# Second batch's four gate projections in a stage of their own, as a 2x2 block product with seven multiplications

## The chip, the cores and the metric

One core of one Trainium2 chip. Matmuls run on TensorE (PE in the profile), elementwise work on VectorE (DVE), ScalarE (ACT) and GpSimd (POOL); SyncE (SP) only issues DMAs. The metric is device microseconds of one execution, as the median of several; the profile is of one execution.

## The reference

Two independent inputs x of 1024 positions x 1024 channels (here: batch 0 and batch 1) go through one layer. The input is normalised and multiplied by one large projection; the result is cut into the sections fv (Fourier branch), fg (its gate), three parts of hv (Hyena branch), hg (its gate) and mg (two merge gates).

```python
xn = rmsnorm(x, g_pre)
p = xn @ w_in
fv, fg, hv, hg, mg = jnp.split(p, [...], axis=-1)
...
y_f = (fz * jax.nn.silu(fg)) @ w_fourier_out
hv = short_conv(hv, w_short)
v, x1, x2 = jnp.split(hv, 3, axis=-1)
...
for n, gate in enumerate((x1, x2)):
    z = gate * long_conv(z, kf[:, n], hyena_d[n])
y_h = (z * jax.nn.silu(hg)) @ w_hyena_out
g_f, g_h = jnp.split(jax.nn.sigmoid(mg + b_merge), 2, axis=-1)
out = (g_f * y_f + g_h * y_h) @ w_out
return x + rmsnorm(out, g_post)
```

The short convolution has width 3 over the positions; the long convolution has a filter as long as the sequence, computed by a small network from the positions, and is done by a Fourier transform of twice the length. Everything is in float32.

## The kernel before

**Precision and matmuls.** A float32 operand is split into two rounded parts, high and low (`split`, L168: ScalarE rounds the high part, VectorE or GpSimd subtracts it). A product is three matmuls, high x high, high x low and low x high (`mm3`, L365), accumulated in a PSUM tile of 128 x 512. All go through `mm` (L192), so the profile shows them under L193 and tells them apart by the PSUM tile's name; subtractions and other two-operand work stand under L181, the three-operand form under L177, the roundings under L171.

**Phases.** `phase_fourier` computes the Fourier branch of both batches and stores the normalised, transposed input in DRAM (`d_x`: 8 tiles of 128 channels x 1024 positions) and the branch's result in `d_fz`. `phase_main` computes the filters' spectra for 8 channel tiles and 2 orders (`filter_taps`, `filter_spectrum`), filling TensorE in between with gate projections of batch 0, and then calls `branches`. `phase_out` does the output projections.

**A projection** (`inproj`, L707) makes one channel tile of 128 output channels for all 1024 positions: two PSUM tiles (`pin0`, `pin1`, 512 positions each), contraction over 8 input tiles, three matmuls each, 48 in all. The weight comes in two halves of 256 KB by SP's queue, is rounded by ScalarE (`wh`) and the rest is subtracted by GpSimd (`wl`). The moving operands are the input's parts `xh0` to `xh7` and `xl0` to `xl7`, loaded by `load_x` (L694) once for each batch; each of these 16 tiles exists once, so batch 1's are loaded when batch 0's last projection has read them. Sections 1 to 3 are the convolution inputs v, x1 and x2, section 0 is the Fourier gate, 4 the Hyena gate, 5 and 6 the two merge gates.

**The branches** (`branches`, L886). For each batch there are 16 steps (n, c): long convolution n of channel tile c, in the order (0,0), (0,1), (1,0), (0,2), (1,1) ... (1,7). A step has a short convolution `conv` (L723: a projection, two scaled copies on ScalarE, four three-operand instructions on VectorE), two of them where n is 0; then `conv_front` (L757: two sums, eight transposes `tph`, the butterfly of VectorE work with its splits `bh`, `bl`); then `conv_back` (L771), which for four groups of frequencies does the forward matmuls (`pX`, four or twelve), VectorE's product with the filter spectrum (`t`, two of 128 x 512; `y`, two of 128 x 256; the split `yh`, `yl`) and twelve inverse matmuls (`pT`), and then joins the groups (`S`, `T1s`, `U`, `T0s`, `ez`, `q`, `yc`); and `gate` (L844), the product with x1 or x2 and the filter's norm `invn`. The result z of n = 1 goes to DRAM (`d_sh`). The x tiles have four buffers, so projections can run ahead of the convolutions by a few steps.

**The gate projections.** Batch 0's stand mostly between the filter computations (`spill_gate`, L739, which stores section 5 and 6 as they are, and section 0 as silu times `d_fz`, in `d_g`). In the branches batch 0 has only section 4 for channel tiles 6 and 7 left. Batch 1 has all of them in the branches: section 4 in `gates` (L904), where GpSimd multiplies x2 by silu of the projection ahead of the convolution, and sections 0, 5 and 6 by `spill_gate` behind each step with n = 1. These are 32 projections.

**Order.** A scheduler orders each engine's instructions at build time from a model of their times; each engine then runs its list in order, waiting on semaphores.

**Output phase** (`phase_out`, L940): for each batch and half of the positions, `operand` loads and splits the eight f tiles (`d_g[b][0]`) and h tiles (`d_sh[b]`), and 8 x 24 matmuls each for `pyf` and `pyh`, the merge gates and the last projection (`po`) follow. The first unit's f tiles are loaded into the pools `sp` and `op`, the others into the tiles of the input x.

Of the kernel before, what the change touches and what calls it, by code (L numbers as in the profile page):

```python
# [16 lines left out]
P = 128  # L17
# [144 lines left out]
class K:  # L162
# [28 lines left out]

    def mm(self, out, lhsT, rhs, start, stop):  # L192
        self.nc.tensor.matmul(out, lhsT, rhs, start=start, stop=stop)  # L193

# [170 lines left out]
    def mm3(self, out, L_, R_, start, stop):  # L365

        self.mm(out, L_[0], R_[0], start, False)
        self.mm(out, L_[0], R_[1], False, False)
        self.mm(out, L_[1], R_[0], False, stop)

# [400 lines left out]
    def conv_back(self, n, ct, B, ws):  # L771
# [3 lines left out]
        for g, pairs in GROUPS:  # L775
# [22 lines left out]
            for r in range(2):  # L798
                for i, pr in enumerate(pairs):
# [12 lines left out]
                    else:  # L812
                        out = T4[:, 1:3]
                        R = [ci[:, hl, o:o + 2 * P].rearrange("p (a b) -> p a b", a=2) for hl in range(2)]
                    self.mm3(out, w, R, i == 0, i == 1)

# [69 lines left out]
    def branches(self, nb, nct, ws):  # L886

        nc = self.nc  # L890
        steps = []
# [12 lines left out]
        def gates(i):  # L904
            b, n, c = steps[i]
            x = self.conv(2 + n, c, ws, f"x{n + 1}")
            if n:
                early = b == 0 and c < NH
                ps = None if early else self.inproj(4, c)
                for q in range(2):  # L910
                    sg = self.wp.tile([P, 512], F32, tag="gt", name="sg", bufs=3)
                    if early:
                        nc.sync.dma_start(sg, self.d_g[0][4][c][:, 512 * q:512 * q + 512])
                    nc.scalar.activation(sg, sg if early else ps[q], AF.Silu)
                    self.mul("pool", x[:, 512 * q:512 * q + 512], x[:, 512 * q:512 * q + 512], sg)
            X[i] = x
        B = front(0)
        gates(0)
        for i, (b, n, c) in enumerate(steps):
# [13 lines left out]
            if b == 0 and NF <= c:  # L933
                self.spill_gate(0, 0, c, ws)
            if b:
                for sec in (0, 5, 6):
                    self.spill_gate(b, sec, c, ws)


    def phase_out(self):  # L940
# [5 lines left out]
        with ExitStack() as es:  # L946
            pool = lambda n: es.enter_context(tc.tile_pool(name=n, bufs=1, reuse_waits="tile"))
            oc, sp, op = pool("oc"), pool("sp"), pool("op")
            wo = {}
            self.nw = 0  # L950

            def operand(i, nm, k):


                b, half = units[i]
                src = (self.d_sh[b] if nm == "h" else self.d_g[b][0])[k][:, 512 * half:512 * half + 512]
                if nm == "f" and i == 0:
                    h = sp.tile([P, 512], F32R, tag=f"mh{k}", name=f"sf{k}", bufs=1)
                    if k % 2 == 0:
                        self.pair = op.tile([P, 2, 512], F32R, tag="xo"[k // 2 % 2], name="sl", bufs=2)  # L960
                    l = self.pair[:, k % 2]
                    r = l.bitcast(F32)
                    nc.sync.dma_start(r, src)
                    self.split(h, l, r, "dve", "act")
                    return h, l
                t = xp.tile([P, 2, 512], F32R, tag=f"x{'l' if nm == 'h' else 'h'}{k}", name=f"s{nm}{k}", bufs=1)
                r = t[:, 1].bitcast(F32)
# [46 lines left out]
            for i, (b, half) in enumerate(units):  # L1014
# [20 lines left out]
                for tt in range(4):  # L1035
                    c = slice(P * tt, P * tt + P)
                    row = 512 * half + P * tt
                    x = op.tile([P, D], F32, tag="x", name="xr", bufs=2)
                    nc.sync.dma_start(x, a[f"x{b}"][row:row + P, :])
# [4 lines left out]
                          for n in range(2)]  # L1044
                    o = op.tile([P, D], F32, tag="o", name="o", bufs=2)
                    for n in range(2):
# [63 lines left out]
def _body(tc, a):  # L1110
    with ExitStack() as ctx:
        k = K(tc, a)
        k.setup(ctx)
        k.phase_fourier()
        k.open_x(ctx)
        k.phase_main()
        k.phase_out()

# [20 lines left out]
```

## Time and profile before

| | us |
|---|---|
| median of 3 runs | 2515.86 (2510.67 to 2516.3) |
| the profiled execution | 2514.28 |
| its span, first to last instruction | 2512.5 |
| Fourier phase and filters, to the first branches | about 0 to 750 |
| branches of batch 0, to the load of batch 1's x | about 750 to 1125 |
| branches of batch 1 with its 32 gate projections | about 1125 to 1970 |
| output phase | 1969.8 to 2512.5 |

How to read the rows: a group's row has line, engine, operation, output<-inputs, shapes and count, then busy time and mean ns of one, then the engine's idle time just before these instructions and what ended it. A window's row has start:end, its length, then busy time (and instruction count) of PE, PEld (weight loads, which overlap matmuls), DVE, ACT and POOL, the granted TensorE clock as a share of full speed, the DMA share and GB/s. A timeline row has start, duration, and the operation; rows of equal instructions that follow each other are merged (x2), and successive instructions overlap a little at their ends.

### The profile page before, as it was taken

The numbers are of one execution on the slowest core, as the hardware profiler recorded it, in microseconds if no ns is written. First come the engines' busy times: TensorE is split into PE (matmuls) and PEld (weight loads), VectorE is DVE, ScalarE is ACT, GpSimd is POOL, SyncE is SP. The second block draws the span as 40 slices with busy tenths as digits, with TensorE's granted clock in tenths as the row PEclk, the third lists the DMA queues.
The fourth block names the chain that finished last, engine by engine and source line by source line (L and its number), as shares of the span: only waits on it lengthen the run. The fifth ranks groups of instructions, "written<-read, shape, count | busy, mean of one in ns | idle before, by whom it ended". The sixth has DMA issues, their size and how long they took to land.

```text
span 2512.5 us, 36976 instructions
## 1 busy us (share of the span) xinstructions
PE 2455.3 (98%) x13412; PEld 2127.8 (85%) x13412; DVE 1853.9 (74%) x3811; ACT 1042.1 (41%) x1950; POOL 543.7 (22%) x472
## 2 busy tenths in 40 slices
PE   6999999999989999999999999999999999999998
PEld 6998888888878888888888888888888778888887
DVE  7786788887789999999997584774856654555544
ACT  6546566566633333334333232232322542424231
POOL 1331223122212332222222212122121210102010
PEclk9999999999989999999999999999999999999999
DMA  7636534333322222233222332223223863545441
GB/s 269 207 105 220 181 134 140 129 124 128 126 82 82 89 91 78 76 97 131 83 90 78 94 89 87 95 68 100 93 70 111 273 204 132 175 148 177 147 144 53
DMA packets 152942, 313.99 MB, mean 125 GB/s; under 512 B 18022, under 2 KB 32583, under 8 KB 152376
## 3 DMA queue, kind: packets, MB, share of 16 engines
q1 hardware_dynamic: 139100, 262.02, 32.1%
q0 software_dynamic: 13472, 49.60, 6.1%
q8 instruction: 105, 1.72, 0.3%
q14 instruction: 77, 0.63, 0.1%
q10 hardware_dynamic: 188, 0.02, 0.0%
HBM read 229.78 MB, written 81.79 MB: 124 GB/s over the span
## 4 chain that ended last, share of the span: by engine, by line
PE 81%; DVE 8%; DMA 5%; ACT 4%; issue 2%; POOL 0%; SPq 0%; DVEq 0%; ACTq 0%; POOLq 0%
PE pin L193 42%; PE pT L193 7%; PE po L193 7%; PE pyh L193 7%; PE pX L193 7%; PE pyf L193 5%; PE pfv L193 2%; PE pXf L193 1%; PE tph L767 1%; DVE kt L177 1%; ACT ex L626 1%; DMA wfv<-in_w_fv 1%; DMA g<-d_g 1%; PE tpx L193 1%; DVE fO L181 1%
## 5 line engine op out<-in xcount | busy, mean ns | idle before, releaser
L193 PE MATMUL pin<-xh,wh 128*128 128x512 f32 x1792 | 701.4, 392 | 1.8 <-DVE x L177 1.1
L193 PE MATMUL pin<-xh,wl 128*128 128x512 f32 x1792 | 701.9, 392 | 0.7 <-POOL wl L181 0.7
L193 PE MATMUL pin<-xl,wh 128*128 128x512 f32 x1792 | 701.5, 392 | 0.0
L181 POOL TENSOR_TENSOR wl<-wr,wh 128x512 fp32r<-128x512 f32 x224 | 367.2, 1640 | 1291.1 <-ACT wh L171 1199.8
L171 ACT CAST wh<-wr 128x512 fp32r<-128x512 f32 x352 | 217.5, 619 | 480.7 <-issue 193.3
L193 PEld LDWEIGHTS pin<-xh,wl 128*128 128x128 f32 x1792 | 337.7, 188 | 64.3 <-POOL wl L181 1.0
L193 PEld LDWEIGHTS pin<-xh,wh 128*128 128x128 f32 x1792 | 337.5, 188 | 64.0 <-DVE x L177 1.4
L193 PEld LDWEIGHTS pin<-xl,wh 128*128 128x128 f32 x1792 | 337.7, 188 | 62.6
L193 PE MATMUL pT<-cinv,yh 128*128 128x256 f32 x1024 | 192.4, 282 | 0.0
L181 DVE TENSOR_TENSOR t<-pX,k 128x512 f32<-128x512 f32 x256 | 163.7, 678 | 14.2 <-PE pX L193 13.3
L193 PEld LDWEIGHTS pT<-cinv,yh 128*128 128x128 f32 x1024 | 164.1, 190 | 9.4
L171 ACT CAST yh<-y 128x512 fp32r<-128x512 f32 x128 | 79.5, 621 | 206.8 <-DVE y L181 187.4
L193 PE MATMUL pyh<-sh,wh 128*128 128x512 f32 x512 | 158.9, 392 | 2.7 <-ACT wh L171 2.7
L193 PE MATMUL pX<-bh,cfwd 128*128 128x256 f32 x768 | 161.5, 286 | 0.0
L193 PE MATMUL pyf<-sf,wh 128*128 128x512 f32 x448 | 143.9, 391 | 3.3 <-ACT wh L171 3.3
L193 PE MATMUL pT<-cinv,yl 128*128 128x256 f32 x512 | 145.1, 283 | 0.0
L193 PEld LDWEIGHTS pX<-bh,cfwd 128*128 128x128 f32 x768 | 127.2, 191 | 2.4
L177 DVE SCALAR_TENSOR_TENSOR x<-pin,wsh,x 128x512 f32<-128x512 f32 (+1 forms) x128 | 89.5, 738 | 48.5 <-ACT x L730 48.5
L181 DVE TENSOR_TENSOR wl<-wr,wh 128x512 fp32r<-128x512 f32 x128 | 87.6, 685 | 48.6 <-ACT wh L171 48.0
L171 ACT CAST bh<-b 128x512 fp32r<-128x512 f32 x144 | 88.4, 619 | 77.2 <-DVE b L181 37.1
L181 DVE TENSOR_TENSOR yl<-y,yh 128x512 fp32r<-128x512 f32 x128 | 102.9, 804 | 20.0 <-ACT yh L171 19.1
L181 DVE TENSOR_TENSOR bl<-b,bh 128x512 fp32r<-128x512 f32 x144 | 108.3, 754 | 12.6 <-ACT bh L171 12.5
(253 smaller groups left out, 4628.7 us busy)
## 6 DMA issues: line engine op xcount, KB each, us to landing
wr<-in_w_in SPq DMA_DIRECT2D x224, 256.0 KB, 2.7
d_g<-gt SPq DMA_DIRECT2D x108, 256.0 KB, 2.4
k<-d_k SPq DMA_DIRECT2D x96, 256.0 KB, 2.7
wr<-in_w_fo POOLq DMA_DIRECT2D x64, 256.0 KB, 3.4
g<-d_g SPq DMA_DIRECT2D x64, 256.0 KB, 2.9
wr<-in_w_ho POOLq DMA_DIRECT2D x64, 256.0 KB, 3.2
d_k<-kt SPq DMA_DIRECT2D x48, 256.0 KB, 2.0
k<-d_k SPq DMA_DIRECT2D x32, 384.0 KB, 3.2
```

The costliest lines, as they stand in the source:

```text
L171: self.rounded = nc.scalar.copy(h, src)
L177: self.nc.vector.scalar_tensor_tensor(out, a, s, b, op0=op0, op1=op1)
L181: e.tensor_tensor(out, a, b, op=op)
L193: self.nc.tensor.matmul(out, lhsT, rhs, start=start, stop=stop)
L626: nc.scalar.activation(ex[:, i], dec, AF.Exp, scale=self.vec[:, q:q + 1])
L767: nc.tensor.transpose(tp[:, q * P:(q + 1) * P], eo[:, e, q], self.ident)
```

## The change

The 32 gate projections of batch 1 leave the branches. Four of them (`PLAIN`: sections 5 and 6, channel tiles 0 and 1) are done as before by `spill_gate`, ordered behind the last inverse matmul of the last long convolution (`self.ended`). The other 28 go to a new stage, `phase_gates`, between `phase_main` and `phase_out`, as 14 jobs of one section and two channel tiles each.

A job is the 2x2 block product C = A B, where A is the weight (two channel tiles by two halves of the 1024 input channels) and B is the input (two halves of the channels by two halves of the positions). It uses a form of Winograd's with seven block products in place of eight: A11 B11, A12 B21, S1 T1, S2 T2, S3 T3, S4 B22 and A22 T4, with S1 = A21 + A22, S3 = A11 + A21, S2 = S1 + A11, S4 = S2 + A12 and T1 = B11 - B12, T3 = B12 - B22, T2 = -T1 - B22, T4 = T2 + B21. One block product (`times`) is 4 input tiles x 3 matmuls. Sums and splits of the weights (`prepare`) are done on VectorE and ScalarE for each job, the next job's ahead of the current one's last two products; the weights come through GpSimd's queue in two DMAs of 512 KB. T1 to T4 are made once, from `d_x`, before the first job; B's own blocks are the x tiles already there. Partial results that several outputs share stay in PSUM and are added to, after ScalarE has copied them (`kept`: m1, u and v). `keep_in_program_order` holds the products in the order in which they are written.

In a job of section 4 or 0 the result goes through silu and is multiplied by `d_sh` or `d_fz`; so batch 1's z is no longer gated in the branches, and its gated form is in `d_g[1][4]`, where `operand` now reads it. In the output phase the first unit's f tiles 0 to 3 are loaded into the x tiles and 4 to 7 into a new pool `ox`, which also holds the tiles of the last projection that were in `op`.

```diff
@@ -189,8 +189,9 @@
     def mul(self, eng, out, a, b):
         self.tt(eng, out, a, b, MUL)
-    def mm(self, out, lhsT, rhs, start, stop):
-        self.nc.tensor.matmul(out, lhsT, rhs, start=start, stop=stop)
+    def mm(self, out, lhsT, rhs, start, stop, shared=False):
+        return self.nc.tensor.matmul(out, lhsT, rhs, start=start, stop=stop, skip_group_check=shared)
     def setup(self, ctx):
@@ -366,7 +367,7 @@
         self.mm(out, L_[0], R_[0], start, False)
         self.mm(out, L_[0], R_[1], False, False)
-        self.mm(out, L_[1], R_[0], False, stop)
+        return self.mm(out, L_[1], R_[0], False, stop)
     def pfv(self, p, e, m, k, W, fo):
         r, c0 = m // 2, P * (m % 2)
@@ -812,7 +813,7 @@
                     else:
                         out = T4[:, 1:3]
                         R = [ci[:, hl, o:o + 2 * P].rearrange("p (a b) -> p a b", a=2) for hl in range(2)]
-                    self.mm3(out, w, R, i == 0, i == 1)
+                    self.ended = self.mm3(out, w, R, i == 0, i == 1)
             def tt(name):
                 return ws.tile([P, 512], F32, tag="tt", name=name, bufs=4)
@@ -887,7 +888,7 @@
-        nc = self.nc
+        tc, nc = self.tc, self.nc
         steps = []
         for b in range(nb):
             steps.append((b, 0, 0))
@@ -904,8 +905,8 @@
         def gates(i):
             b, n, c = steps[i]
             x = self.conv(2 + n, c, ws, f"x{n + 1}")
-            if n:
-                early = b == 0 and c < NH
+            if n and b == 0:
+                early = c < NH
                 ps = None if early else self.inproj(4, c)
                 for q in range(2):
                     sg = self.wp.tile([P, 512], F32, tag="gt", name="sg", bufs=3)
@@ -932,9 +933,123 @@
             nc.sync.dma_start(self.d_sh[b][c], z)
             if b == 0 and NF <= c:
                 self.spill_gate(0, 0, c, ws)
-            if b:
-                for sec in (0, 5, 6):
-                    self.spill_gate(b, sec, c, ws)
+        with tc.issue_after(self.ended.ins):
+            for sec, c in self.PLAIN:
+                self.spill_gate(1, sec, c, ws)
+    PLAIN = [(5, 0), (5, 1), (6, 0), (6, 1)]
+    def phase_gates(self):
+        tc, nc, a = self.tc, self.nc, self.a
+        wp, b = self.wp, 1
+        jobs = [(s, c) for c in range(0, 8, 2) for s in (0, 4, 5, 6) if (s, c) not in self.PLAIN]
+        with ExitStack() as es:
+            pool = lambda n: es.enter_context(tc.tile_pool(name=n, bufs=1, reuse_waits="tile"))
+            gs, gw, gr = pool("gs"), pool("gw"), pool("gr")
+            def prepare(sec, c):
+                r = gr.tile([P, 4, 512], F32, tag="raw", name="wraw", bufs=2)
+                for i in range(2):
+                    nc.gpsimd.dma_start(r[:, 2 * i:2 * i + 2].rearrange("p a b -> p (a b)"), a["w_in"][sec, c + i])
+                s = gw.tile([P, 4, 512], F32, tag="sum", name="wsum", bufs=1)
+                A = {}
+                def parts(n, pool, tags, src, bufs):
+                    h, l = [pool.tile([P, 4, P], F32R, tag=t, name=t, bufs=bufs) for t in tags]
+                    self.split(h.rearrange("p a b -> p (a b)"), l.rearrange("p a b -> p (a b)"), src, "dve", "act")
+                    A[n] = h, l
+                parts("11", wp, ("wh", "wl"), r[:, 0], 2)
+                parts("12", wp, ("wh", "wl"), r[:, 1], 2)
+                self.add("dve", s[:, 0:2], r[:, 2].unsqueeze(1).to_broadcast([P, 2, 512]), r[:, 3::-3])
+                self.add("dve", s[:, 2], s[:, 0], r[:, 0])
+                parts("s2", gw, ("s2h", "s2l"), s[:, 2], 1)
+                h, l = [gw.tile([P, 2, 4, P], F32R, tag=t, name=t, bufs=1) for t in ("s13h", "s13l")]
+                f = lambda t: t.rearrange("p s a b -> p s (a b)")
+                self.split(f(h), f(l), s[:, 0:2], "dve", "act")
+                A["s1"], A["s3"] = (h[:, 0], l[:, 0]), (h[:, 1], l[:, 1])
+                self.add("dve", s[:, 3], s[:, 2], r[:, 1])
+                parts("s4", gw, ("s4h", "s4l"), s[:, 3], 1)
+                parts("22", gw, ("a2h", "a2l"), r[:, 3], 1)
+                return A
+            A = prepare(*jobs[0])
+            TH, TL = [], []
+            for k in range(4):
+                r = gr.tile([P, 4, 512], F32, tag="raw", name="xraw", bufs=2)
+                for i in range(2):
+                    nc.sync.dma_start(r[:, 2 * i:2 * i + 2].rearrange("p a b -> p (a b)"), self.d_x[b][k + 4 * i])
+                s = gw.tile([P, 4, 512], F32, tag="sum", name="xsum", bufs=1)
+                self.sub("dve", s[:, 0::2], r[:, 0:2], r[:, 1::2])
+                self.stt("dve", s[:, 1], s[:, 0], -1.0, r[:, 3], MUL, SUB)
+                self.add("dve", s[:, 3], s[:, 1], r[:, 2])
+                h, l = [gs.tile([P, 4, 512], F32R, tag=f"{t}{k}", name=f"{t}{k}", bufs=1) for t in ("th", "tl")]
+                self.split(h, l, s, "dve", "act")
+                TH.append(h)
+                TL.append(l)
+            own = lambda k, n: (slice(0, 512), slice(512, 1024))[n]
+            block = lambda i, n: [(self.xh[4 * i + k][:, own(k, n)], self.xl[4 * i + k][:, own(k, n)]) for k in range(4)]
+            B11, B21, B22 = block(0, 0), block(1, 0), block(1, 1)
+            T1, T2, T3, T4 = [[(TH[k][:, j], TL[k][:, j]) for k in range(4)] for j in range(4)]
+            def times(p, A, B, first):
+                for k in range(4):
+                    h, l = A[0][:, k], A[1][:, k]
+                    for j, (w, x) in enumerate(((h, B[k][0]), (h, B[k][1]), (l, B[k][0]))):
+                        m = self.mm(p, w, x, first and k + j == 0, k + j == 5, True)
+                        if k + j == 0:
+                            tc.keep_in_program_order(m)
+            def out(sec, c, n, p, q, op):
+                s = slice(512 * n, 512 * n + 512)
+                t = wp.tile([P, 512], F32, tag="gt", name="gt", bufs=3)
+                if q is not None:
+                    self.tt("dve", t, p, q, op)
+                if sec in (0, 4):
+                    f = gw.tile([P, 512], F32, tag="f", name="fz", bufs=3)
+                    nc.sync.dma_start(f, (self.d_sh if sec else self.d_fz)[b][c][:, s])
+                    nc.scalar.activation(t, p if q is None else t, AF.Silu)
+                    self.mul("dve", t, t, f)
+                elif q is None:
+                    nc.scalar.copy(t, p)
+                nc.sync.dma_start(self.d_g[b][sec][c][:, s], t)
+            def kept(p, own=False):
+                t = gw.tile([P, 512], F32, tag="u", name="u", bufs=1) if own else wp.tile([P, 512], F32, tag="w", name="m", bufs=2)
+                nc.scalar.copy(t, p)
+                return t
+            def first(A):
+                pa, pb = self.psum("mm", 4, "pg"), self.psum("X", 2, "pg")
+                times(pa, A["11"], B11, True)
+                m1 = kept(pa)
+                times(pb, A["12"], B21, True)
+                return pa, pb, m1
+            pa, pb, m1 = first(A)
+            for i, (sec, c) in enumerate(jobs):
+                out(sec, c, 0, pb, m1, ADD)
+                times(pa, A["s2"], T2, False)
+                u = kept(pa, True)
+                pc = self.psum("T", 2, "pg")
+                times(pc, A["s3"], T3, True)
+                times(pa, A["s1"], T1, False)
+                v = kept(pa)
+                out(sec, c + 1, 1, pc, v, SUB)
+                last = (A, pa, pc, u)
+                if i + 1 < len(jobs):
+                    A = prepare(*jobs[i + 1])
+                    pa, pb, m1 = first(A)
+                A_, pa_, pc_, u = last
+                times(pa_, A_["s4"], B22, False)
+                out(sec, c, 1, pa_, None, None)
+                times(pc_, A_["22"], T4, False)
+                out(sec, c + 1, 0, pc_, u, SUB)
     def phase_out(self):
@@ -945,7 +1060,7 @@
         units = [(b, half) for b in range(NB) for half in range(2)]
         with ExitStack() as es:
             pool = lambda n: es.enter_context(tc.tile_pool(name=n, bufs=1, reuse_waits="tile"))
-            oc, sp, op = pool("oc"), pool("sp"), pool("op")
+            oc, sp, op, ox = pool("oc"), pool("sp"), pool("op"), pool("ox")
             wo = {}
             self.nw = 0
@@ -953,17 +1068,11 @@
                 b, half = units[i]
-                src = (self.d_sh[b] if nm == "h" else self.d_g[b][0])[k][:, 512 * half:512 * half + 512]
-                if nm == "f" and i == 0:
-                    h = sp.tile([P, 512], F32R, tag=f"mh{k}", name=f"sf{k}", bufs=1)
-                    if k % 2 == 0:
-                        self.pair = op.tile([P, 2, 512], F32R, tag="xo"[k // 2 % 2], name="sl", bufs=2)
-                    l = self.pair[:, k % 2]
-                    r = l.bitcast(F32)
-                    nc.sync.dma_start(r, src)
-                    self.split(h, l, r, "dve", "act")
-                    return h, l
-                t = xp.tile([P, 2, 512], F32R, tag=f"x{'l' if nm == 'h' else 'h'}{k}", name=f"s{nm}{k}", bufs=1)
+                src = (self.d_g[b][0] if nm == "f" else self.d_g[b][4] if b else self.d_sh[b])[k][:, 512 * half:512 * half + 512]
+                if nm == "f" and i == 0 and k >= 4:
+                    t = ox.tile([P, 2, 512], F32R, tag="xo"[k % 2], name=f"sf{k}", bufs=2)
+                else:
+                    t = xp.tile([P, 2, 512], F32R, tag=f"x{'l' if nm == 'h' else 'h'}{k}", name=f"s{nm}{k}", bufs=1)
                 r = t[:, 1].bitcast(F32)
                 nc.sync.dma_start(r, src)
                 self.split(t[:, 0], t[:, 1], r, "dve", "act")
@@ -1035,14 +1144,14 @@
                 for tt in range(4):
                     c = slice(P * tt, P * tt + P)
                     row = 512 * half + P * tt
-                    x = op.tile([P, D], F32, tag="x", name="xr", bufs=2)
+                    x = ox.tile([P, D], F32, tag="x", name="xr", bufs=2)
                     nc.sync.dma_start(x, a[f"x{b}"][row:row + P, :])
                     ss = op.tile([P, 2], F32, tag="ss", name="ss", bufs=2)
                     s1 = op.tile([P, 1], F32, tag="s1", name="s1", bufs=2)
                     rs = op.tile([P, 1], F32, tag="rs", name="rs", bufs=2)
                     ps = [self.psum("mm", 4, f"po{n}") if tt < 2 else self.psum(("X", "T")[n], 2, f"po{n}")
                           for n in range(2)]
-                    o = op.tile([P, D], F32, tag="o", name="o", bufs=2)
+                    o = ox.tile([P, D], F32, tag="o", name="o", bufs=2)
                     for n in range(2):
                         s = slice(512 * n, 512 * n + 512)
                         for k in range(8):
@@ -1114,6 +1223,7 @@
         k.phase_fourier()
         k.open_x(ctx)
         k.phase_main()
+        k.phase_gates()
         k.phase_out()
```

## The prediction

> **What bounds the kernel now.** First the page: the span, the engines' shares, the slices and the chain that ended last.
>
> ```profile
> span 2512.5 us, 36976 instructions
> PE 2455.3 (98%) x13412; PEld 2127.8 (85%) x13412; DVE 1853.9 (74%) x3811; ACT 1042.1 (41%) x1950; POOL 543.7 (22%) x472
> PE   6999999999989999999999999999999999999998
> DVE  7786788887789999999997584774856654555544
> PE 81%; DVE 8%; DMA 5%; ACT 4%; issue 2%; POOL 0%; SPq 0%; DVEq 0%; ACTq 0%; POOLq 0%
> ```
>
> TensorE (PE) holds 81% of the chain, so work taken from it is worth its full time. But VectorE (DVE) stands at nine tenths from slice 12 to slice 20: those are the branches of the first batch (about 750 to 1130 us), which have hardly any gate projections between their convolutions. The second batch's branches, with all its gate projections among them, leave DVE half idle. Then the busy times of stretches: a steady piece of the first batch's branches, the second batch from the point where the two programs part to the first matmul of the output phase, and the output phase.
>
> ```profile
> core 0: us, PE busy (x) PEld busy (x) DVE busy (x) ACT busy (x) POOL busy (x), PEclk, DMA share, GB/s
> 800.00:1100.00 300.00, 300.00 (x1802) 267.02 (x1801) 290.96 (x588) 110.37 (x186) 81.86 (x43) 1.00 0.27 84
> 1217.40:1969.80 752.40, 752.13 (x4093) 652.45 (x4092) 524.31 (x965) 230.57 (x393) 172.15 (x122) 1.00 0.30 95
> 1969.80:2512.50 542.70, 528.30 (x2305) 433.56 (x2303) 279.30 (x550) 201.66 (x360) 66.05 (x123) 0.99 0.49 157
> ```
>
> In the first batch both engines are full at once: DVE works 290.96 of 300 us. The timeline gives the marks, and the real price of a matmul.
>
> ```profile
> 1217.19 0.39 PE L193 MATMUL pin<-xh,wh 128*128 128x512 f32 x1
> 1217.42 0.60 PE L767 MATMUL tph<-ident,eo 128*128 128x128 f32 x4
> ...
> 1948.31 0.28 PE L193 MATMUL pT<-cinv,yl 128*128 128x256 f32 x1
> ...
> 1969.77 0.39 PE L193 MATMUL pyf<-sf,wh 128*128 128x512 f32 x1
> ...
> 1974.98 0.39 PE L193 MATMUL pyf<-sf,wl 128*128 128x512 f32 x1
> ```
>
> The last two rows are the first and the 24th of 24 matmuls in a row: 5.21 us / 23 = 0.2265 us each from start to start (the 0.39 us of a row is a pipelined length). The row at 1217.19 is the first matmul of the second batch's first gate projection; up to it TensorE's order is the same in both programs. The last inverse-transform matmul (pT) starts at 1948.31.
>
> **The change, part by part.**
>
> *Matmuls removed.* An ordinary projection of one channel tile is 48 matmuls. Before, 32 gate projections lie in the stretch: 1536 matmuls. After: 4 plain ones (192) and 14 jobs of 7 products x 12 (84 each), 1176 together. 168 fewer, x 0.2265 = 38.1 us less TensorE work. Were TensorE the bound throughout, that would be the gain.
>
> *Matmuls moved.* In the order of the changed program none of the 1368 stands among the branches: the 4 plain projections come behind the last pT, then the 14 jobs. So until the last pT, TensorE has 752.4 - 1536 x 0.2265 = 404.5 us of work left. DVE's work there is not reduced. These are the rows for it, first the first batch's piece (800 to 1100 us), then the stretch from 1217.4 to 1969.8:
>
> ```profile
> L181 DVE TENSOR_TENSOR t<-pX,k 128x512 f32<-128x512 f32 x82 | 52.5, 678 | 1.1 <-PE pX L193 0.8
> L181 DVE TENSOR_TENSOR bl<-b,bh 128x512 fp32r<-128x512 f32 x30 | 22.4, 748 | 2.1 <-ACT bh L171 2.1
> L177 DVE SCALAR_TENSOR_TENSOR x<-pin,wsh,x 128x512 f32<-128x512 f32 x21 | 15.5, 740 | 0.7 <-ACT x L730 0.7
> L177 DVE SCALAR_TENSOR_TENSOR x<-yc,invn,x 128x1024 f32<-128x1024 f32 x10 | 15.1, 1511 | 0.0
> L177 DVE SCALAR_TENSOR_TENSOR v<-pin,wsh,v 128x512 f32<-128x512 f32 x10 | 7.4, 735 | 0.0
> ```
>
> ```profile
> L181 DVE TENSOR_TENSOR t<-pX,k 128x512 f32<-128x512 f32 x130 | 83.1, 678 | 12.9 <-PE pX L193 12.6
> L177 DVE SCALAR_TENSOR_TENSOR x<-pin,wsh,x 128x512 f32<-128x512 f32 x28 | 20.8, 742 | 44.9 <-ACT x L730 44.9
> L181 DVE TENSOR_TENSOR gt<-gt,fz 128x512 f32<-128x512 f32 x16 | 13.0, 811 | 8.0 <-ACT gt L752 8.0
> L177 DVE SCALAR_TENSOR_TENSOR v<-pin,wsh,v 128x512 f32<-128x512 f32 x12 | 8.9, 745 | 5.5 <-ACT v L730 5.5
> L181 DVE TENSOR_TENSOR sl<-sl,sf 128x512 fp32r<-128x512 f32 x8 | 6.2, 820 | 0.9 <-ACT sf L171 0.9
> L181 DVE TENSOR_TENSOR wl<-wr,wh 128x512 fp32r<-128x512 f32 x2 | 1.4, 687 | 2.2 <-ACT wh L171 2.2
> L181 DVE TENSOR_TENSOR sh<-sh 128x512 fp32r<-128x512 f32 x1 | 0.7, 692 | 4.0 <-ACT sh L171 4.0
> ```
>
> Each long convolution has 8 rows t, each short convolution four rows on pin (two of 512 columns, two of 511, so twice the counts shown). The piece holds 82 / 8 = 10.25 long and (21 + 10) / 2 = 15.5 short ones. At four times about 0.737 us a short one takes 2.95 us, all of them 45.7; the rest, (290.96 - 45.7) / 10.25, is 23.9 us for a long one. After 1217.4 there remain 130 / 8 = 16.25 long and (28 + 12) / 2 = 20 short ones, in both programs: 16.25 x 23.9 + 20 x 2.95 = 447 us of DVE work. Part of it comes behind the last pT, from S to the last product with invn:
>
> ```profile
> 1929.21 0.69 DVE L181 TENSOR_TENSOR bl<-b,bh 128x512 fp32r<-128x512 f32 x1
> ...
> 1949.26 0.68 DVE L181 TENSOR_TENSOR S<-T1s,pT 128x512 f32<-128x512 f32 x1
> ...
> 1956.21 1.27 DVE L177 SCALAR_TENSOR_TENSOR x<-yc,invn,x 128x1024 f32<-128x1024 f32 x1
> ```
>
> That is 1949.26 to 1957.48, 8 us (the row bl is for the bounds below), so 439 us must pass before the last pT can. At the piece's utilisation of 0.97 that is 453 us. TensorE needs only 404.5: DVE takes over as the bound and TensorE waits about 50 us, in one place above all. In the new order the last projection is followed by 214 pT matmuls, 4.46 convolutions' worth (48 each), with no projection between them; before, gate projections stood there.
>
> At the very end a single convolution is left. Its price is read from the last one of before:
>
> ```profile
> 1927.12:1948.40 21.28, 21.28 (x134) 19.21 (x133) 14.33 (x25) 6.55 (x12) 3.12 (x3) 1.00 0.28 87
> ```
>
> DVE worked 14.33 of 21.28 us though its own chain was all that it had: 7 us of waiting for ScalarE (ACT) and TensorE in turn. I add these 7: last pT at 1217.4 + 460.
>
> *Bounds of the 460.* Below: GpSimd (POOL) slows DVE rows by contention. Isolated rows are shorter than the piece's means (bl 0.69 against 0.748, three a convolution; the product with invn 1.27 against 1.511); with as much again in smaller ones that is some 0.7 us a convolution, 11 us in all. With no idle at all: 439 - 11 = 428. Above: the work at the rate of the second batch now, 524.3 less the rows gt, sl, wl and sh, is 503 us, less 8: 495. I stay near the piece, which has the new branches' mix of work; GpSimd has 43 instructions there in 10.25 convolutions and will have fewer.
>
> *The plain four and the jobs.* 192 x 0.2265 = 43.5 us, then 1176 x 0.2265 = 266.4 us. What must hide under them is priced by these rows:
>
> ```profile
> L181 DVE TENSOR_TENSOR xl<-xl,xh 128x1024 fp32r<-128x1024 f32 x7 | 9.0, 1290 | 0.0
> L171 ACT CAST xh<-xl 128x1024 fp32r<-128x1024 f32 x16 | 16.7, 1053 | 5.2 <-DMA xl<-d_x 5.2
> L171 ACT CAST wh<-wr 128x512 fp32r<-128x512 f32 x352 | 217.5, 619 | 480.7 <-issue 193.3
> ...
> L748 ACT COPY gt<-pin 128x512 f32<-128x512 f32 x76 | 44.2, 582 | 44.7 <-PE pin L193 44.6
> ```
>
> Entry: after the last pT, DVE does its 8 us, the first job's weights (two instructions of 1.29 and five of 0.69: 6 us) and four groups of T operands. A group has 1024, 512 and 512 columns of sums (1.29 + 2 x 0.69), then ScalarE rounds 2048 columns (2 x 1.05) while DVE waits, since the sum tile is single, then DVE subtracts 2048 (2 x 1.29): 7.3 us, four of them 29. With two weight splits of 0.69 that is 45 us. The cover is 43.5 plus the first two products of 2.7 us, which need no T: 49. If loads come late this is the place; the raw tiles lie over the inverse tables, free from the last pT on. In the steady state a job is 84 x 0.2265 = 19.0 us of TensorE against 9.4 to 12.2 us of DVE (five splits and two sums of 0.69, a split and a sum of 1.29, three to seven output rows) and 6.5 to 8.3 of ScalarE. Each kept copy (0.58) stands between two uses of its accumulator with a product of 2.7 us over it; behind a late copy queue the splits of the next job. I take 6 us of stalls for entry and jobs, 0 to 20 as bounds (0.5 us at each of 42 copies would be 21).
>
> *Output phase.* Its matmuls are the same. The first unit's eight f operands now load into the tiles of x 0 to 3, whose last use lies eight products (22 us) before the jobs' end, and into a small pool. The 14.4 us that TensorE idles there (542.70 - 528.30) stay, +-5.
>
> *Sum.* 460 + 43.5 + 266.4 + 6 = 776 against 752.4: +23.5 us. Span 2512.5 + 23.5 = 2536; this execution took 2514.28, so 2538, with the shown runs' median 1.6 above it at 2515.86 and within their scatter.
>
> **The clock.** One idle of TensorE before the branches shows what a gap costs:
>
> ```profile
> 714.47 2.04 PE L193 MATMUL pXf<-b,cfw 128*128 128x128 f32 x8 [5.73 <-DVE b L181]
> ...
> 715.00:720.00 5.00, 4.05 (x20) 3.76 (x18) 5.00 (x17) 3.29 (x7) 0.00 (x0) 0.50 0.00 0
> 720.00:725.00 5.00, 4.36 (x11) 3.23 (x11) 4.86 (x12) 2.99 (x7) 0.00 (x0) 0.50 0.20 79
> ```
>
> After 5.73 us of waiting the granted clock was 0.50 for some ten microseconds. [...]
>
> **The rivals.**
> 1. *DVE at its floor.* If it runs without gaps and with little contention, the last pT comes at 428 and stalls are 2: 428 + 43.5 + 266.4 + 2 = 740, -12.5: 2502. For it: DVE idled only 9 us in the 300. Against: the thin tail. The full 38 us (2476) would need DVE to end by 404.5, under its floor. With 6 us of stalls the two programs tie at 436 us; under 429 the change is a gain, from 429 to 444 no change.
> 2. *Jobs starved* at entry or by the in-order ScalarE queue: 20 us of stalls in place of 6: 2552. Against: DVE and ScalarE are each under two thirds busy there.
> 3. *Half clock in the tail.* Less the 912 matmuls of the short convolutions' own 19 projections, a long convolution has (404.5 - 912 x 0.2265) / 16.25 = 12.2 us of matmuls, the tail 54, twice as long then; most hides under DVE, but the last convolution's stand in its chain: 12, and some 4 more for the first plain projection: 2554. For it: the rows above. Against: with two convolutions in flight most gaps are only a few microseconds.
>
> **How the numbers follow.** Forecast 0.59; rival 1 0.07; its middle piece (no change) 0.12; rival 2 0.12; rival 3 0.10. Within 0.3%, 7.5 us, nothing can be told apart: faster 0.07, same 0.12, slower 0.81. The likeliest time is 2538. The range goes from 2510 (the last pT at 432, between the floor of 428 and the 439 without idle) to 2568 (the last pT at 477, halfway to the upper bound, and 20 us of stalls).
>
> **What would show it.** Right: DVE above 95% from 1217 until the last pT near 1677; TensorE in gaps before it, mostly behind the last convolution projection; jobs in 267 to 275 us; the output phase in 543. Wrong: TensorE full until the last pT (then DVE was cheaper), the last pT before 1655, gaps of several microseconds between products, or a changed time before 1217.

## The result, and the profile after

The changed kernel took 2547.77 us (median of 4 runs, 2544.22 to 2551.97) against 2516.08 before (4 runs, 2510.67 to 2516.64): ratio 1.0131, 95% interval 1.011 to 1.0153. Slower, as forecast, by 32 us where 22 to 24 were forecast. The page of the profiled execution after:

```profile
span 2547.1 us, 36978 instructions
PE 2447.1 (96%) x13244; PEld 2118.5 (83%) x13244; DVE 1959.4 (77%) x4011; ACT 1083.0 (43%) x2006; POOL 481.4 (19%) x428
...
PE   6999999999989999999999999689999999999998
DVE  7786788887889999999999999975555555545543
PEclk9999999999989999999999999789999999999999
```

TensorE did 168 matmuls less and yet the span grew by 34.6 us. VectorE now stands at nine tenths through both batches' branches, to slice 25, and in slice 25 TensorE falls to 6 and its clock to 7. The stretches of after, cut where the prediction cut them: parting point to the last pT, its last part alone, the four plain projections, the jobs, the jobs without their ends, one piece of the way out of them, and the output phase.

```profile
1218.20:1686.90 468.70, 432.10 (x2557) 385.59 (x2556) 451.97 (x927) 151.90 (x258) 76.69 (x39) 0.93 0.24 73
1595.00:1686.90 91.90, 63.70 (x351) 57.55 (x352) 86.39 (x187) 22.65 (x38) 0.00 (x0) 0.72 0.18 54
1686.90:1734.30 47.40, 45.43 (x193) 36.84 (x193) 32.27 (x34) 17.14 (x21) 15.14 (x10) 0.97 0.57 195
1734.30:2011.10 276.80, 270.20 (x1178) 222.76 (x1176) 146.97 (x207) 106.23 (x178) 15.25 (x29) 0.99 0.45 148
1745.00:1985.00 240.00, 240.00 (x1061) 198.70 (x1060) 128.00 (x182) 90.83 (x150) 12.06 (x23) 1.00 0.41 138
2000.00:2005.00 5.00, 0.97 (x3) 0.80 (x3) 3.65 (x6) 3.27 (x6) 1.07 (x2) 0.87 0.39 129
2011.10:2547.10 536.00, 525.18 (x2305) 431.63 (x2303) 277.30 (x547) 198.00 (x354) 65.98 (x123) 1.00 0.49 158
```

VectorE (the third busy time) works 451.97 of the 468.70 us up to the last pT, and 86.39 of the 91.90 in the thin tail, where TensorE is busy for 63.70 at a clock of 0.72. Inside the jobs TensorE is full: 240 us hold 1061 matmuls, 0.2262 us each. So the jobs cost no time there beyond their matmuls; the time is lost before the jobs and at their two ends. Against the terms of the forecast, in us:

| | forecast | measured |
|---|---|---|
| start of the stretch, against before | 0 | +0.8 |
| parting point to the last pT | 460 | 468.7 |
| plain projections, jobs, stalls | 315.9 | 47.4 + 276.8 = 324.2 |
| output phase, against before's 542.7 | 0 | -6.7 |
| span, against before's 2512.5 | +23.5 | +34.6 |

The jobs were forecast at 267 to 275 us and took 276.8. In the 64 us by which the first stretch is longer than TensorE's own 404.5, TensorE idles for 36.6 us (468.70 - 432.10); in the other 27.6 it counts as busy, with matmuls that take longer at the lower clock: from one pX of 128 x 256 to the next it is 0.21 us at a granted clock of 0.50 (1614.33 to 1614.54) and 0.12 at 1.00 (1588.70 to 1588.82).

### The profile page after: what moved, and what is told of

Its sections match the earlier page's. It is cut to its first block, busy times and chain, and to the rows that moved or that the text cites. A ratio compares the mean times of both kernels' runs of the same rounds, so it can differ in the third digit from the quotient of the medians.

```text
span 2547.1 us, 36978 instructions
## 1 busy us (share of the span) xinstructions
PE 2447.1 (96%) x13244; PEld 2118.5 (83%) x13244; DVE 1959.4 (77%) x4011; ACT 1083.0 (43%) x2006; POOL 481.4 (19%) x428
## 5 line engine op out<-in xcount | busy, mean ns | idle before, releaser
L194 PE MATMUL pin<-xh,wl 128*128 128x512 f32 x1344 | 527.2, 393 | 2.2 <-POOL wl L181 2.2
L194 PE MATMUL pin<-xh,wh 128*128 128x512 f32 x1344 | 526.9, 394 | 2.0 <-DVE x L177 1.1
L194 PE MATMUL pin<-xl,wh 128*128 128x512 f32 x1344 | 527.0, 392 | 0.0
L181 POOL TENSOR_TENSOR wl<-wr,wh 128x512 fp32r<-128x512 f32 x168 | 312.5, 1861 | 1048.3 <-ACT wh L171 966.3
L171 ACT CAST wh<-wr 128x512 fp32r<-128x512 f32 x296 | 182.4, 618 | 317.1 <-PE pin L194 144.3
L194 PEld LDWEIGHTS pin<-xh,wl 128*128 128x128 f32 x1344 | 254.0, 189 | 49.4 <-POOL wl L181 3.0
L194 PEld LDWEIGHTS pin<-xh,wh 128*128 128x128 f32 x1344 | 253.9, 189 | 49.1 <-DVE x L177 1.3
L194 PEld LDWEIGHTS pin<-xl,wh 128*128 128x128 f32 x1344 | 254.0, 189 | 46.5
L194 PEld LDWEIGHTS pX<-bh,cfwd 128*128 128x128 f32 x768 | 130.7, 197 | 10.9 <-DVE t L181 4.8
L194 PE MATMUL pX<-bl,cfwd 128*128 128x256 f32 x384 | 113.0, 294 | 2.4 <-DVE bl L181 2.4
L194 PEld LDWEIGHTS pyh<-sh,wh 128*128 128x128 f32 x512 | 95.9, 188 | 22.9 <-ACT wh L171 3.2
```

Of the source, the lines that this page charges most:

```text
L171: self.rounded = nc.scalar.copy(h, src)
L181: e.tensor_tensor(out, a, b, op=op)
L194: return self.nc.tensor.matmul(out, lhsT, rhs, start=start, stop=stop, skip_group_check=shared)
```

## The experiments

All times are medians; each ratio is against the kernel before, run on the same chip in the same session, where that kernel's median was 2516.5 for the first four, 2519.5 for the next four and 2520.4 for the last two. The profiled executions reach the parting point up to 13 us apart (the second short convolution of batch 1 gives the shift), so stretches are counted from there.

**1. Moving alone.** The 28 projections stay behind the branches but are ordinary ones:

```diff
     def phase_gates(self):
-        jobs = [...]
-        ...
+        for c in range(8):
+            for sec in (0, 4, 5, 6):
+                if (sec, c) not in self.PLAIN:
+                    self.spill_gate(1, sec, c, None)
```

(`spill_gate` multiplies section 4 by `d_sh`.)

> Moves the projections as the change does, but computes all 28 of them in the ordinary way (48 matmuls each) behind the branches; the seven-product jobs are gone. Theory (VectorE bounds the second batch's branches once the projections have left; the stage behind them is bound by TensorE): the last pT comes as in the changed kernel, 468 to 470 us after the parting point, then 1536 x 0.2265 = 348 us of projections, and the entry and exit gaps of the jobs (about 10 us) mostly go: 2547.8 + 38 - 10 = 2576, 2570 to 2588. Rival A (the jobs themselves, with their sums, splits and kept copies, are what costs): near or under the time of before, 2516 to 2530.

Measured: 2580.84 us, ratio 1.0253 (1.0215 to 1.0292), within the expected 2570 to 2588. The stretches up to the last pT and of the projections behind it:

```profile
1218.90:1686.60 467.70, 429.92 (x2557) 383.05 (x2556) 451.52 (x927) 151.86 (x258) 76.59 (x39) 0.94 0.24 73
1686.60:2036.20 349.60, 349.60 (x1537) 289.45 (x1537) 46.27 (x53) 78.02 (x134) 82.93 (x67) 1.00 0.40 130
```

The first stretch is that of the changed kernel within 1 us, so what lengthens it is the moving and not the jobs. The second is 349.6 us for 348 us of matmuls: ordinary projections have no entry or exit gap. The changed kernel takes 324.2 there. The seven products therefore earn 25.4 us of their 38.1 in this stage; the other 12.7 go at the ends of the jobs. About 5.7 of these come back behind it, since the output phase takes 541.7 us in this run and 536.0 in the changed kernel. Against before, moving costs 64 us and the block product gives back 33 by the medians.

**2 and 3. VectorE relieved in the second batch, after and before.**

```diff
-            self.split(h, l, b, "dve", "act")
+            if self.lean:            # second batch
+                nc.scalar.copy(h, b)
+                l = h
+            else:
+                self.split(h, l, b, "dve", "act")
...
-            self.split(yh, yl, Y, "dve", "act")
+            # likewise, yl = yh
```

> The changed kernel with VectorE relieved in the second batch's long convolutions: the subtractions that make bl and yl are left out there and the high part is fed to the matmul in place of the low one, so TensorE's work stays and 114 subtractions of about 0.7 us (80 us) go. Theory: VectorE falls from 452 to about 375 us, under TensorE's 404.5, so the last pT comes 410 to 425 us after the parting point in place of 469, and the time falls by 45 to 58: 2490 to 2503, under the time of before. Rival A (the jobs): no more than 10 us gained, 2538 to 2548. Rival B (half clock in the thin tail is the main loss): the tail has less VectorE work but as many gaps; 10 to 25 us gained, 2523 to 2538.

> The same relief (bl and yl of the second batch left out) in the kernel before. Theory: TensorE is the bound there, full for 752 of 752.4 us, so nothing is gained: 2516 within 4 us, and under 8 even if the last step's chain gets shorter. A theory in which VectorE also bounds the kernel before would give 2440 to 2490.

Measured: the changed kernel with the relief 2498.61 us, ratio 0.9934 (0.9897 to 0.997), 49 us less than without; the kernel before with it 2511.74, ratio 0.998 (0.9968 to 0.9992), 5 us less. The stretch to the last pT of the changed kernel, then that from the parting point to the output phase of the kernel before, both with the relief:

```profile
1220.20:1638.10 417.90, 405.53 (x2556) 366.64 (x2555) 387.37 (x815) 150.69 (x258) 67.56 (x39) 0.99 0.27 81
```

```profile
1217.10:1968.20 751.10, 751.10 (x4091) 653.02 (x4090) 453.94 (x853) 231.54 (x394) 165.34 (x122) 1.00 0.30 96
```

The same subtractions were worth 51 us up to the last pT where VectorE had been the bound (468.7 to 417.9, near TensorE's own 404.5), and 1.3 us where TensorE was full (752.4 to 751.1). Both times lie in the ranges expected for VectorE as the bound after, and TensorE as the bound before. What the rest of run 3's 5 us is was not traced. The relief cannot tell VectorE from the clock, though: with it the stretch's clock rises from 0.93 to 0.99 as well. Run 4 and VectorE's busy time in the tail tell these two apart.

**4. Extra work in the tail.** Four projections done once more among the last steps:

```diff
             nc.sync.dma_start(self.d_sh[b][c], z)
+            if b:
+                for sec, ct in self.FILL.get(c, ()):
+                    self.spill_gate(1, sec, ct, ws)
...
+    FILL = {4: [(5, 2)], 5: [(5, 3), (6, 2)], 6: [(6, 3)]}
```

> The changed kernel with four projections done twice: sections 5 and 6 of channel tiles 2 and 3 once more as ordinary projections among the last steps of the second batch's branches (192 extra matmuls, 43.5 us of TensorE work), all else as it is. Theory: TensorE waits 64 us there for VectorE, so the extra work costs next to nothing: 2548, from 2540 (some gaps closed, the clock stays up) to 2558 (contention from eight more weight splits on GpSimd). Rival A or a TensorE-bound branch: 2588 to 2592. Rival B (half clock): the filled gaps keep the clock up, 10 to 20 us gained, 2528 to 2538.

Measured: 2558.22 us, ratio 1.0163 (1.0126 to 1.0201), just at the upper end of the expected 2540 to 2558: 43.5 us of matmuls cost 10.5.

```profile
1217.70:1697.30 479.60, 458.19 (x2747) 408.32 (x2746) 452.81 (x927) 160.66 (x274) 94.08 (x47) 0.97 0.26 80
```

Three quarters cost no time. The stretch is 10.9 us longer, TensorE's idle in it fell by 15 (36.6 to 21.4), and TensorE's busy time grew by only 26 us (432.10 to 458.19) for 43.5 us of matmuls, at a granted clock of 0.97 in place of 0.93. VectorE's work is the same as in the changed kernel (452.81 and 451.97); its idle grew from 17 to 27 us. The waits show on what, first in the changed kernel, then here (engine, line, what it waited for, us in total, times, longest):

```profile
DVE S L181 <- PE pT L194: 3.5, 5, 1.5
```

```profile
DVE S L181 <- PE pT L194: 10.4, 7, 5.7
```

Projections that the scheduler put ahead of a pT made VectorE wait: from 1605 to 1616 us, just before the longest of these waits (5.7 us) ends at 1618.21, a projection's matmuls stand among the pT that S needs. The clock was 0.97 in place of 0.93 and the last pT came no earlier for it, so the lower clock was not what held it.

**5 to 10. Projections moved back into the branches.** The same `FILL`, now in place of jobs:

```diff
-        jobs = [... if (s, c) not in self.PLAIN]
+        jobs = [... if (s, c) not in self.PLAIN + sum(self.FILL.values(), [])]
...
# 5: FILL = {4: [(5, 2)], 5: [(5, 3), (6, 2)], 6: [(6, 3)]}
# 6: FILL = {3: [(0, 0)], 4: [(0, 1), (5, 2)], 5: [(5, 3), (6, 2)], 6: [(6, 3)]}
# 8, 10: FILL = {4: [(0, 0)], 5: [(0, 1), (5, 2)], 6: [(5, 3), (6, 2), (6, 3)]}
# 9: FILL = {3: [(0, 0)], 4: [(0, 1)], 5: [(0, 2), (5, 2), (0, 3)], 6: [(5, 3), (6, 2), (6, 3)]}
# 7 (as 6) and 10 besides, in the butterfly:
-            self.split(h, l, b, "dve", "act")
+            self.split(h, l, b, "pool" if self.relief else "dve", "act")
```

> The same four projections (sections 5 and 6 of channel tiles 2 and 3) among the last steps of the branches, now in place of the two jobs that made them: 12 jobs remain. Theory: as the run with four done twice (2558.2), less two jobs of 84 x 0.2265 = 19.0 us: 2520, from 2512 to 2526. Rival A (the jobs cost more than their matmuls): the two jobs gone give more than 45 us, under 2510. If the extra projections were not hidden behind VectorE: 2548 + 43.5 - 38 = 2553.

> Six projections among the last steps (two of section 0 besides), 11 jobs remain. Theory: TensorE's wait of 64 us nearly holds six projections (65 us); three jobs less is -57 us; the delay of the last pT, 11 us with four, grows to 15 to 25: 2505 to 2516, against 2516.5 of before: a tie or a small gain. If the filling is free: 2493. If the room ends at four: 2523 or more.

> As the run with six, and VectorE relieved without leaving work out: in the second batch GpSimd makes bl (48 subtractions of about 0.73 us on VectorE, 35 us). [...] Rival: contention and the longer butterfly (1.6 us in place of 0.7) eat it all: equal or slower.

> As the run with six, the six projections one step later each (channel tiles 4, 5 and 6 of the last batch's steps), so that more of them stand in the thin tail and fewer ahead of the last convolution's own projection. Theory: VectorE must not be starved before the tail; if the 11 us delay with four came of projections standing ahead of pT and of the last convolution projection, this is 5 to 10 us faster than the run with six; if it came of contention, within 3 us of it.

> As the late run with six, with eight projections among the last steps (section 0 of channel tiles 2 and 3 besides) and 10 jobs. Theory: with eight, TensorE's own work up to the last pT, 404.5 + 8 x 10.87 = 491.5 us, is above what VectorE needs (about 480), so each projection added now costs its time and the bound is back at TensorE: one job less (-19.0) against up to 21.7 us more, less the idle that it still fills: equal to the late run with six within 6 us (2504 to 2516). If VectorE were still the bound: 19 us faster, 2491.

> The late run with six, with bl of the second batch subtracted by GpSimd. Early placement gained 2.5 us on the last pT by it (6 us in the time). Theory: with six projections TensorE (469.7 us of work) and VectorE (about 453) are nearly even and most idle is the two waiting for each other, so 2 to 6 us come off: 2504 to 2509. If VectorE were the bound alone: 15 us or more.

| run | us | ratio to before (95%) | parting point to last pT |
|---|---|---|---|
| changed kernel | 2547.77 | 1.0131 (1.011 to 1.0153) | 468.7 |
| 5: four | 2521.67 | 1.0015 (1.0003 to 1.0026) | 479 |
| 6: six | 2521.61 | 1.0008 (0.9999 to 1.0018) | 489 |
| 7: six, bl on GpSimd | 2515.54 | 0.9987 (0.9976 to 0.9998) | 487 |
| 8: six, one step later | 2510.17 | 0.9966 (0.9953 to 0.998) | 487 |
| 9: eight, later | 2502.76 | 0.9938 (0.9919 to 0.9956) | 502.5 |
| 10: six, later, bl on GpSimd | 2499.24 | 0.9917 (0.9895 to 0.9939) | 480.4 |

With four the expectation held. With six it was missed (2505 to 2516 expected): the last pT came 10 us later again, and the stage behind it became only 12.5 us shorter (280.7 to 268.2) where a job is worth 19.0. Run 7 was expected 5 to 20 us under run 6, at 2488 to 2505, with VectorE as the bound. It is 6 us under run 6, at the low end, but its time missed the range, which had been counted from a faster run 6.

One step later, the same six are 11 us faster, where 5 to 10 were expected if placement ahead of pT was the cause, and under 3 if it was contention. That does not show placement: only 2.3 us of it lie before the last pT. Behind it the stage takes 260.3 us in place of 268.2. In run 6 TensorE idles there for 10.0 us, of which 3.6 are a wait for the first job's wl from VectorE; in run 8 it idles for 5.0 and that wait is gone. The other 3 us are busy time. These are single profiled executions, and no run separates the causes.

With eight a tie was expected (2504 to 2516): 2502.76 is better. The last pT came 15.9 us later, and the stage behind it was 22.1 us shorter with one job less. Run 10 is faster than both kernels, and faster than expected (2504 to 2509). Up to the last pT it gained 6.2 us, the upper end of the 2 to 6 expected, but most of that is not less waiting: VectorE's busy time fell by 4.5. The rows show how little that is of the work handed over: VectorE's groups in run 8, then run 10's busy times of the stretch and its groups of VectorE and GpSimd.

```profile
L181 DVE TENSOR_TENSOR y<-t,t 128x256 f32<-128x256 f32 x132 | 52.4, 436 | 0.2
L181 DVE TENSOR_TENSOR yl<-y,yh 128x512 fp32r<-128x512 f32 x66 | 46.7, 708 | 4.0 <-ACT yh L171 3.6
L181 DVE TENSOR_TENSOR bl<-b,bh 128x512 fp32r<-128x512 f32 x48 | 35.1, 733 | 3.4 <-ACT bh L171 3.4
...
L181 DVE TENSOR_TENSOR eo<-x 128x512 f32<-128x512 f32 x16 | 10.3, 682 | 0.1
```

```profile
1225.40:1705.80 480.40, 473.89 (x2845) 418.94 (x2844) 454.52 (x884) 163.51 (x282) 176.49 (x99) 1.00 0.27 86
```

```profile
L181 DVE TENSOR_TENSOR y<-t,t 128x256 f32<-128x256 f32 x132 | 68.4, 557 | 0.4
L181 DVE TENSOR_TENSOR yl<-y,yh 128x512 fp32r<-128x512 f32 x66 | 49.9, 757 | 3.4 <-ACT yh L171 3.3
L181 DVE TENSOR_TENSOR eo<-x 128x512 f32<-128x512 f32 x16 | 14.0, 912 | 0.0
...
L181 POOL TENSOR_TENSOR bl<-b,bh 128x512 fp32r<-128x512 f32 x48 | 75.2, 1573 | 72.3 <-ACT bh L171 69.8 <-DVE yl L181 2.4
```

The 35 us of bl left VectorE, but with GpSimd busy for 75 us more the rows y, yl and eo grew by 23; VectorE's busy time fell only from 459 (run 8) to 454.5. Runs 6 and 7 agree: 34 us of bl left, and VectorE's busy time fell from 457.5 to 454.1. The rest of the ratio's gain lies outside that stretch and was not explained.

## Why the prediction was right, point by point

*The bound.* Shown: VectorE takes over in the second batch's branches (runs 2 and 3: 51 us there, 1.3 before), because the moving took TensorE's other work away (run 1). The 38.1 us of matmuls did go, and TensorE lost twice as much again: 64.2 us before the last pT (468.7 - 404.5) and 14.3 behind it. That the time came within 10 us of the forecast is in part luck: the last pT and the stage behind it were each 8 to 9 us longer than forecast, and the output phase 6.7 shorter.

*VectorE's work* was mis-sized: 439 us up to the last pT, measured 452. The prices held: each row's count in the stretch after, at that row's busy time in the piece and with the piece's share of overlap, gives 456. The count was off, that of the joins (from S to the product with invn). The piece holds 10 of them, but was counted as 10.25 convolutions by its 82 rows t. Scaled by 16.25 / 10.25, that makes 15.9 joins, and one was taken off for the end: 14.9. The trace after has 16 to 17 before the last pT:

```profile
L181 DVE TENSOR_TENSOR t<-pX,k 128x512 f32<-128x512 f32 x130 | 83.2, 678 | 0.5
L177 DVE SCALAR_TENSOR_TENSOR x<-yc,invn,x 128x1024 f32<-128x1024 f32 x17 | 23.7, 1395 | 0.0
...
L181 DVE TENSOR_TENSOR S<-T1s,pT 128x512 f32<-128x512 f32 x16 | 10.9, 680 | 3.5 <-PE pT L194 3.5
```

At the forecast's 8 us each, one to two joins are 9 to 17 us, which covers the 13. The contention bound was no help: isolated rows were approached (1.395 us for the product with invn against 1.511; 15 of its 17 rows have no GpSimd work beside them and take 1.27, the other two 2.31 and 2.32), and the work still came out higher.

*Idle* was 14 + 7 = 21 us in the forecast, and 16.7 measured; the chain of the last convolution is in it. This took back 4 of the 13 us.

*Entry and exit* were the other mis-sized term: 6 us of stalls, 14.3 measured (324.2 - 309.9). In 8.6 of them TensorE idles (324.2 - 45.43 - 270.20); in the other 5.7 it counts as busy beyond the 309.9 us of its matmuls (45.43 + 270.20 = 315.6), with granted clocks of 0.97 over the plain four and 0.93 over the last 26 us of the jobs. The entry had been named as the place. The sums of T waited for their loads (two of VectorE's rows), and TensorE, a little later, for the low parts of its weights, from GpSimd in the last plain projection and from VectorE in the first job:

```profile
1721.49 1.23 DVE L181 TENSOR_TENSOR xsum<-xraw 128x1024 f32<-128x1024 f32 x1 [3.52 <-DMA xraw<-d_x]
...
1729.94 1.23 DVE L181 TENSOR_TENSOR xsum<-xraw 128x1024 f32<-128x1024 f32 x1 [1.51 <-DMA xraw<-d_x]
```

```profile
PE pg L194 <- DVE wl L181: 2.6, 1, 2.6
...
PE pin L194 <- POOL wl L181: 1.7, 1, 1.7
```

The longest wait is at the exit, and it has rival 2's cause, the in-order queue of ScalarE. In the last job no product of a next job stands between a kept copy and the use of its accumulator. The copy v (its tile is named m) stands in ScalarE's list behind the roundings of the output phase's f operands (`sf`), and the first of these waits for its load. ScalarE's rows, TensorE's, then the stretch:

```profile
2000.54 0.62 ACT L171 CAST sf<-sf 128x512 fp32r<-128x512 f32 x1 [4.97 <-DMA sf<-d_g]
...
2003.48 0.57 ACT L1025 COPY m<-pg 128x512 f32<-128x512 f32 x1
```

```profile
2004.11 0.80 PE L194 MATMUL pg<-xh,s4h 128*128 128x512 f32 x1 [4.03 <-ACT m L1025]
```

```profile
1985.00:2011.10 26.10, 22.07 (x92) 17.84 (x90) 12.36 (x20) 11.92 (x22) 2.14 (x4) 0.93 0.66 206
```

Every run that keeps jobs has this wait, from 2.8 us (run 4) to 5.6 (run 6); no run was made that puts the copy ahead. The copies of the jobs before cost nothing, the 240 us piece being full. Rival 2 as a whole, 20 us, came to 14.3. Part of the exit's loss has changed sides: the output phase is 6.7 us shorter than before and 5.7 shorter than in run 1, which has no jobs.

*Half clock in the tail* came, 0.72 on the mean, but cost little: VectorE was busy for 86.39 of the 91.90 us, so at most 5.5 us can be laid to it and the tail's other waits together. Before the tail VectorE idles for another 11 us, but the clock is 0.99 there. Rival 3's other 4 us, at the first plain projection, were the author's estimate, and no run shows them as a term: the whole excess of that stage is 3.9 us (47.4 - 43.5), 2.0 of it idle (47.40 - 45.43).

*VectorE at its floor* did not come: it would have needed the last pT at 429, and VectorE's work alone was 452.

## What to carry to other kernels

Fewer matmuls help only while the matmuls stand where TensorE is the bound: before taking filler work out of a stage, sum what the other engine needs there, and compare. Here 348 us of matmuls left a stage in which VectorE works for 452 us, where TensorE's rest was 404.5. When such a stage is filled again, look at which instruction of the in-order list the filler stands in front of: extra projections made VectorE wait longer for pT (run 4: S for 10.4 us in place of 3.5), and six of them gained nothing over four until they stood one step later (runs 5, 6 and 8). In such a list a load that is waited for also holds what stands behind it, as the last job's copy at the exit (TensorE waited 4.03 us for it); and work handed from VectorE to GpSimd is priced by VectorE's busy time afterwards, not by the rows that it loses (run 10: 4.5 us less, for rows of 35.1).

## What the runs showed of the hardware that was not expected

In one part of the tail the clock fell to half among gaps that were all short (2.56 us at most). TensorE's rows with their waits in the changed kernel's tail, then the stretches:

```profile
1596.34 0.39 PE L194 MATMUL pX<-bh,cfwd 128*128 128x256 f32 x1 [2.56 <-DVE t L181]
...
1605.20 0.80 PE L194 MATMUL pT<-cinv,yh 128*128 128x256 f32 x2 [1.72 <-ACT yh L171]
1606.63 2.07 PE L194 MATMUL pX<-b,cfw 128*128 128x128 f32 x8 [0.63 <-DVE b L181]
1609.40 0.55 PE L194 MATMUL pX<-bh,cfwd 128*128 128x256 f32 x1 [0.70 <-DVE t L181]
1613.52 0.58 PE L194 MATMUL pX<-bl,cfwd 128*128 128x256 f32 x1 [1.11 <-DVE bl L181]
```

```profile
1605.00:1610.00 5.00, 3.48 (x12) 2.67 (x12) 5.00 (x13) 0.77 (x2) 0.00 (x0) 0.50 0.00 0
1610.00:1615.00 5.00, 3.89 (x17) 3.59 (x18) 5.00 (x14) 2.99 (x5) 0.00 (x0) 0.50 0.18 52
```

No wait in these two stretches is over 1.72 us, and none in the 20 us before them over 2.56; TensorE counts as busy for 70 to 78%, yet the clock stays at 0.50. The tail has one long gap too, and behind it the clock came back sooner:

```profile
1655.56 1.75 PE L768 MATMUL tph<-ident,eo 128*128 128x128 f32 x7 [9.51 <-DVE eo L181]
```

```profile
1655.00:1660.00 5.00, 4.44 (x24) 4.22 (x25) 2.89 (x7) 1.44 (x3) 0.00 (x0) 0.60 0.13 46
1660.00:1665.00 5.00, 4.77 (x41) 4.57 (x40) 5.00 (x17) 2.56 (x5) 0.00 (x0) 1.00 0.00 0
```

After 9.51 us of waiting the clock was at 1.00 again within 5 us, with TensorE busy for 89 to 95%. So the ten microseconds at 0.50 that the forecast shows behind a shorter wait, of 5.73 us, are no fixed time of return: TensorE was busy there for only 81 to 87%, with waits of 0.94 and 0.64 us between. What takes the clock down and what brings it back was not shown.

GpSimd's price for VectorE was larger than expected: 75 us of GpSimd work took back about 30 of the 35 us that it relieved, by VectorE's busy time (runs 8 and 10; 31 of 34 in runs 6 and 7).
